# The second score matmul on 128 rows in place of 64, its low operand padded with zeros

## The chip, the cores and the metric

The kernel runs on one core of one Trainium2 chip. The metric is the time of one execution on the device, in microseconds (us); lower is better. Times are given as the median of several executions. A core has five engines that run their own queues of instructions: TensorE (PE in the profile; PEld is its weight loads), VectorE (DVE), ScalarE (ACT), GpSimd (POOL) and SyncE (SP, which only issues transfers here).

## The reference

One step of a hybrid decoder layer, for a prompt of 2048 tokens and a group of 8 × 8 sample tokens, with 1024 channels, in float32. Each token is normalised, projected into three parallel branches (attention, a short gated convolution, a spatial MLP on chunks of 128 positions), and the branches are gated, projected back and added to the input. The change touches the attention of the prompt, whose core is this:

```python
def _sink_attend(q, k, v, dist, valid, sinks):
    s = jnp.einsum("...qkgd,...skd->...kgqs", q, k).astype(jnp.float32) * (HEAD_DIM ** -0.5)
    s = s - _alibi_slopes()[:, :, None, None] * dist.astype(jnp.float32)
    s = jnp.where(valid, s, NEG_INF)
    ...
    e = jnp.exp(s - mx)
    prob = e / (e.sum(axis=-1, keepdims=True) + jnp.exp(sink - mx))
    return jnp.einsum("...kgqs,...skd->...qkgd", prob.astype(v.dtype), v)
```

There are 8 query heads in 2 key groups, 64 channels a head, and a block of 128 queries sees the 128 keys of its own block and the 128 of the block before. The contraction of a score is thus over 64 channels.

## The kernel before

The tokens are worked through in four super-blocks (called blocks here) of 4 prompt tiles of 128 tokens; the last takes the 64 sample tokens too, so that its large products run in two chunks of 288 columns instead of one of 512. A block has these phases, in this order: `kv_phase` and `q_phase` (the "natural" products, L285 to L287, tokens on partitions, 256 columns), then the large products with the channels on partitions (L176 to L178) for the attention's gate, `conv_phase`, `chunk_phase` (with a second stretch of natural products and the spatial products, L672 and L673), `gate_phase` and `out_phase`.

To keep float32 precision on a faster matmul type (fp32r), every operand is split: the high part is a cast by ScalarE (L167), the low part the rest by VectorE (L168). A product is then three matmuls, high by high, high by low and low by high. Weights come by transfers from SyncE's queue, and their split is ordered two weight tiles ahead of their use.

Attention is done in units of one query tile and one key group, 8 units in a block, 32 in all. A unit has stages: `queries` (transposes, L421, then the split into `hh` and `ll`), `scores` (L441 and L442), the softmax on VectorE and ScalarE (L444 to L461), `probs` (transposes, L466, and a split) and `values` (L473 and L474). TensorE's order is written by hand: while the large products go on, a counter of weight tiles advances (`tick`), and a stage is put between the products when its time has come (`later`): scores 1.75 weight tiles behind the unit's start, the probabilities at 3.5 and 4, a new unit every 2. So all the stages of a unit stand between the large products of `conv_phase` and its neighbours. VectorE, ScalarE and GpSimd get their order from a scheduler.

A score has its own form of the split. The key tile `kst` holds the high part of a key's 64 channels at partitions 0 to 63 and the low part at 64 to 127 (L331, L332). The high part `hh` of the query stands in both halves, so that L441, over 128 rows, gives high by high and high by low in one matmul. The low part `ll` of the query stands at partitions 0 to 63 only, and L442 adds low by high over these 64 rows. Both write the same stretch of the PSUM tile `sp`, head by head: eight matmuls in a unit, each with 256 key columns (128 in the first two units of block 0, which have no block before them).

`hh` and `ll` are stretches of `rbuf`, two sets of them in turn. `rbuf` takes the buffer with the tag "mh", which the first block's input (`xin`), the spatial operand (`vbuf`) and the high part of the merged branches (`m`, read to the end of `out_phase`) take at other times.

On GpSimd there are the pairs of operations that make 1/rms (`rstd`, L163 and L164: xr for the tokens, kr for the keys, qr for the queries, vr for the MLP) and a few constants. The scaling of the keys, L341 on VectorE, takes kr; L319 on TensorE transposes the result.

Of the kernel before, what the change touches and what calls it, by code (L numbers as in the profile page):

```python
# [16 lines left out]
P = 128  # L17
D = 1024
# [9 lines left out]
WE = 1024  # L28
# Weight units loaded, and split, ahead of their use
RAWS = 3  # L30
AHEAD = 2
# When the side work of an attention unit, and of the spatial products, is emitted:
# delays in weight tiles of the large products
UNIT_EVERY = 2.0
# [3 lines left out]

# Super-blocks of tokens: (first prompt tile, prompt tiles, column chunks, with the sample group)
SBS = [  # L40
# [8 lines left out]
def trunk_kernel(ctx: ExitStack, tc: tile.TileContext, A, O):  # L49
# [27 lines left out]

    # Work that runs beside the large products: each piece is emitted when the
    # products have advanced to its time, counted in weight tiles of 1024 x 128.
    clock = [0.0]  # L80
# [14 lines left out]

# [1 line left out]
    def order():  # L97
# [44 lines left out]

# [1 line left out]
    def const(name):  # L144
# [7 lines left out]

# [1 line left out]
    xh = res.tile([P, KT, TMAX], F32R, name="xh")  # L154
# [6 lines left out]
    def rstd(out, ssq, n, width):  # L161
        """out = (ssq / width + eps) ** -0.5"""
        nc.gpsimd.tensor_scalar(out, ssq, 1.0 / width, EPS, ALU.mult, ALU.add)  # L163
        nc.gpsimd.tensor_tensor(out, out, mhalf[: out.shape[0], :n], ALU.pow)  # L164
# [5 lines left out]
    def gemm_t(ps, w, kts, rh, rl, c0, c1):  # L170
        """ps[m, c0:c1] = w[k, m].T @ r[k, c0:c1], three exact partial products per k tile"""
        wh, wl = w
        o = ps[:, : c1 - c0]
        for k in range(kts):
            ws = slice(k * P, (k + 1) * P)
            nc.tensor.matmul(o, wh[:, ws], rh(k, c0, c1), start=k == 0, stop=False)  # L176
            nc.tensor.matmul(o, wh[:, ws], rl(k, c0, c1), start=False, stop=False)  # L177
            nc.tensor.matmul(o, wl[:, ws], rh(k, c0, c1), start=False, stop=k == kts - 1)  # L178
            if k % 2:
                tick((c1 - c0) / 512 * 0.25)  # L180
# [3 lines left out]
    def t_tiles(j, chunks):  # L184
        """For one 128-column tile of w_in: (psum, c0, c1) of each chunk"""
        w = take("wt", j)
        for c0, c1 in chunks:
            ps = ps_mm()
            gemm_t(ps, w, KT, *xr, c0, c1)
            yield ps[:, : c1 - c0], c0, c1  # L190

# [1 line left out]
    def xrstd(sb):  # L193
        """Pieces that build 1 / rms of the block's tokens, on all partitions"""
        t0, _, chunks, _ = SBS[sb]
        n = chunks[-1][1]
        tiles = [(c, min(c + P, n)) for c in range(0, n, P)]
        st = {"x": res.tile([P, 4 * TMAX], F32, tag="za", name="xbuf")}
        st["r"] = res.tile([P, TMAX], F32, tag="acc", name="acc")[:, :n]
        r = small.tile([P, 8], F32, tag="xr", name="xr")  # L200

        def piece(j, c0, c1):
            w = c1 - c0
            x = st["x"][:w, j % 2 * D:(j % 2 + 1) * D]
            nc.sync.dma_start(x, A["xn"][t0 * P + c0:t0 * P + c1])
            nc.scalar.activation(x, x, AF.Square, accum_out=r[:w, j:j + 1])

        def fin():
            for j0, j1, w in ((0, n // P, P), (n // P, len(tiles), n % P)):
                if w and j1 > j0:  # L210
                    rstd(r[:w, j0:j1], r[:w, j0:j1], j1 - j0, D)

        def spread():
            for t in (tiles[:4], tiles[4:]):
                if t:
                    ps = ps_tp()
                    b = t[0][0]
                    for c0, c1 in t:
                        w = c1 - c0
                        nc.tensor.transpose(  # L220
                            ps[:, c0 - b:c1 - b], r[:w, c0 // P:c0 // P + 1].broadcast_to([w, P]), ident[:w, :w]
                        )
                    nc.scalar.copy(st["r"][:, b:t[-1][1]], ps[:, : t[-1][1] - b])

        return st, [lambda j=j, c=c: piece(j, *c) for j, c in enumerate(tiles)] + [fin, spread]
# [21 lines left out]
    def first_block():  # L247
        """The first block's x, 128 tokens at a time so that the products start early"""
        xin = res.tile([P, 8 * TMAX], F32, tag="mh", name="xin")
        xnat = res.tile([P, 8 * TMAX], F32, tag="ml", name="xnat")  # L250
        r = small.tile([P, 8], F32, tag="xr", name="xr")
        rbuf = res.tile([P, 4 * TMAX], F32, tag="za", name="xrbuf")
        view = lambda t, i: t[:, i * D:(i + 1) * D].rearrange("p (k t) -> p k t", k=KT)  # noqa: E731

# [22 lines left out]

# [1 line left out]
    def natural(o, i, rows, units, n=256):  # L279
        """[rows tokens of tile i, n columns], the columns' weights in two units of 4 k tiles"""  # L280
        ts = slice(i * P, i * P + rows)
# [117 lines left out]

    def attention(sb, qn, abuf, za, br, start, every):  # L400
        """Schedules the block's attention: units of (128 queries, key group), each in stages"""
        t0, ntile, _, _ = SBS[sb]
        rbuf = res.tile([P, 4 * 1024], F32R, tag="mh", name="rbuf")
        sbuf = res.tile([P, 8 * TMAX], F32, tag="ml", name="sbuf")
        state = {}
# [11 lines left out]
        def queries(i, g, b):  # L417
            ps = ps_tp()
            q0 = i * 512 + g * 256
            for a in range(2):  # L420
                nc.tensor.transpose(ps[:, a * P:(a + 1) * P], qn[:, q0 + a * P:q0 + (a + 1) * P], ident)  # L421
            # head 2 a + e of the group has the channels at partitions 64 e
            hh = b["hh"].rearrange("p (a e t) -> p a e t", a=2, e=2)
# [10 lines left out]
        def scores(i, g, b, kbs):  # L434
# [3 lines left out]
            for h in range(4):  # L438
                rhs = kst[:, g, i + kbs[0]: i + 2, :]
                hs = slice(h * P, (h + 1) * P)  # L440
                nc.tensor.matmul(sp[:, h, k0:], b["hh"][:, hs], rhs, start=True, stop=False)  # L441
                nc.tensor.matmul(sp[:, h, k0:], b["ll"][:HD, hs], rhs[:HD], start=False, stop=True)  # L442
            for h in range(4):
# [53 lines left out]
    def sample_attention(samp, sbuf, za, br):  # L497
        """Schedules the attention of the sample group over the cached and the new keys"""
        cv, kc = sbuf[:, 2048:3072], sbuf[:, 3072:4096]
# [5 lines left out]
        def queries():  # L505
            q = samp["q"]
            ps = ps_tp()
            for h in range(8):
                nc.tensor.transpose(
                    ps[0:HD, h * NTS:(h + 1) * NTS], q[h // 4][:, (h % 4) * HD:(h % 4 + 1) * HD], ident[:NTS, :NTS]  # L510
                )
            # columns are (sequence, head of the group, token)
            for g in range(2):
# [108 lines left out]
    def chunk_phase(sb, br, samp_args):  # L622
# [24 lines left out]
        def mixed(i, rows, t, gg):  # L647
            """Times u * silu(z), for the channel groups gg"""
            ts = slice(i * P, i * P + rows)
            t = t[:, gg]  # L650
            nc.vector.tensor_tensor(t, t, suc[:, gg, ts], ALU.mult)
            split(br2[0][:, gg, ts], br2[1][:, gg, ts], t)
# [55 lines left out]
    def keep(new, old):  # L708
        """The rows of a cache that stay in the window"""
        tc.keep_in_program_order(nc.scalar.dma_start(O[new][:, : P - TS, :], A[old][:, TS:, :]))  # L710
# [83 lines left out]

    # spatial weights, transposed and masked: [s, group, t], zero where s > t
    # as (high, low, high) parts side by side
    wsp = consts.tile([P, 4, 3, P], F32R, name="wsp")
    wsd = consts.tile([NTS, 4, NTS], F32, name="wsd")

    def spatial_weights():  # L800
# [6 lines left out]
        nc.scalar.copy(wsp[:, :, 2], wsr)  # L807
        # the sample group's, block-diagonal: [64, group, 64]
        nc.gpsimd.memset(wsd, 0.0)
# [37 lines left out]
def _tiles(w):  # L847
    """[K, M] -> [M / 128, 128 (k), K / 128, 128 (m)] with the last two merged"""
    k, m = w.shape
    return w.reshape(k // P, P, m // P, P).transpose(2, 1, 0, 3).reshape(m // P, P, k)  # L850


def _layout(i):
# [11 lines left out]
    c = {n: w[:, at[j]:at[j + 1]] for j, n in enumerate(names)}  # L865
    # channel tile t of branch A: head t, then head 4 + t
    perm = np.concatenate([np.r_[t * HD:(t + 1) * HD, (4 + t) * HD:(5 + t) * HD] for t in range(4)])
# [9 lines left out]
    nat = [np.concatenate([c["k"], c["v"]], 1), c["q"][:, :256], c["q"][:, 256:], c["vc"][:, :256], c["vc"][:, 256:]]  # L877
    # [chunk, half of k, 128 (k), 4 k tiles, 256 columns]
    a["wn"] = np.stack([x.reshape(2, 4, P, 256).transpose(0, 2, 1, 3) for x in nat]).reshape(10, P, 1024)
# [10 lines left out]
    a["sinkb"] = np.broadcast_to(sk, (P, 8))  # L890
    # sample rows are (sequence mod 4, head of the group, token)
    a["sinks_s"] = np.tile(np.repeat(sk.reshape(2, 4).T, TS, 0), (4, 1))
# [9 lines left out]
    a["cv"] = cv.transpose(1, 0, 2, 3).reshape(P, NS * P)  # L902
    # tables that depend on shapes alone
    a["ident"] = np.eye(P, dtype=f)
# [49 lines left out]
```

## Time and profile before

| | |
|---|---|
| median of 3 runs | 2108.92 us (2108.08 to 2109.45) |
| span of the profiled execution, first to last instruction | 2107.5 us |
| time of the profiled execution outside its span | not recorded by itself; the median is 1.4 us above the span |
| TensorE busy | 2086.3 us, 99% |
| VectorE, ScalarE, GpSimd busy | 50%, 40%, 4% |
| mean granted clock of TensorE | 0.998 |
| matmuls of the scores, L441 and L442 | 128 each |

In the rows of the timeline the first number is the start in us from the beginning of the span, the second the duration in us; then follow the engine, the line, the operation, the output and the inputs. `64*128` in a matmul's row is the rows of the contraction by the columns of the loaded operand, `64x256` the moving operand. Brackets at the end give how long the engine idled ahead of the row and what ended that. Matmuls overlap and their ends are modelled, so their cost is read from start to start. In a row of windows the numbers are the stretch, its length, and the busy time of PE, PEld, DVE, ACT and POOL with instruction counts, then the granted clock, the share of the transfer engines and GB/s. A group's row gives the count, the busy us and the mean ns; one of a single line gives minimum, median and maximum in ns. A row of waits gives who waited for whom, the total in us, the times and the longest.

### The profile page before, as it was taken

How to read it: one execution, taken by the hardware profiler on the slowest of the kernel's cores; microseconds unless marked ns; L12 is line 12 of the kernel's file. 1: busy time of each engine (PE TensorE's matmuls, PEld its weight loads, DVE VectorE, ACT ScalarE, POOL GpSimd, SP SyncE). 2: the span in 40 equal slices, each digit the busy share in tenths (PEclk: the TensorE clock that was granted, in tenths of full speed). 3: DMA queues.
4: the chain of work that ended last, by engine and by line, in shares of the span. 5: the costliest groups of instructions: out<-in, count | busy, mean ns of one | idle time of the engine just before them, and what ended most of it. 6: DMA issues, size and time to landing. Idle time of an engine off the chain costs nothing.

```text
span 2107.5 us, 29115 instructions
## 1 busy us (share of the span) xinstructions
PE 2086.3 (99%) x11703; PEld 1808.5 (86%) x11703; DVE 1059.0 (50%) x1869; ACT 850.9 (40%) x1513; POOL 92.3 (4%) x160
## 2 busy tenths in 40 slices
PE   6999999999999999999999999999999999999999
PEld 6877888888877898888977788888899999999999
DVE  6576263335577444335467625334546852533332
ACT  5665243332566333333366524333346642323230
POOL 2100000000200000000200000000030000000000
PEclk9999999999999999999999999999999999999999
DMA  6222233436222223325422223333622241222233
GB/s 196 84 71 80 84 102 109 125 106 215 81 70 71 90 76 114 117 90 188 128 81 70 81 80 100 120 98 118 205 85 51 51 119 56 63 86 81 86 101 105
DMA packets 85703, 212.36 MB, mean 101 GB/s; under 512 B 18225, under 2 KB 23345, under 8 KB 85553
## 3 DMA queue, kind: packets, MB, share of 16 engines
q1 hardware_dynamic: 85536, 209.53, 32.2%
q8 instruction: 92, 1.51, 0.3%
q10 hardware_dynamic: 32, 0.98, 0.1%
q14 instruction: 43, 0.34, 0.1%
HBM read 201.46 MB, written 10.00 MB: 100 GB/s over the span
## 4 chain that ended last, share of the span: by engine, by line
PE 98%; ACT 1%; DVE 1%; DMA 0%; POOL 0%; issue 0%; SPq 0%; DVEq 0%
PE ps_mm L176 26%; PE ps_mm L177 26%; PE ps_mm L178 26%; PE ps_mm L287 3%; PE ps_mm L286 3%; PE ps_mm L285 3%; PE sp L442 2%; PE sp L441 2%; PE ps_tp L466 1%; PE first L286 1%; PE first L285 1%; PE first L287 1%; PE pv L473 1%; PE pv L474 1%; PE ps_tp L672 0%; PE ps_tp L673 0%
## 5 line engine op out<-in xcount | busy, mean ns | idle before, releaser
L176 PE MATMUL ps_mm<-xh,wh 128*128 128x512 f32 (+1 forms) x2080 | 752.6, 362 | 0.5 <-ACT za L828 0.5
L178 PE MATMUL ps_mm<-xh,wl 128*128 128x512 f32 (+1 forms) x2080 | 740.2, 356 | 0.0
L177 PE MATMUL ps_mm<-xl,wh 128*128 128x512 f32 (+1 forms) x2080 | 740.1, 356 | 0.0
L168 DVE TENSOR_TENSOR wl<-raw,wh 128x1024 fp32r<-128x1024 f32 x376 | 407.4, 1085 | 529.9 <-ACT wh L167 527.7
L167 ACT CAST wh<-raw 128x1024 fp32r<-128x1024 f32 x376 | 353.0, 940 | 763.8 <-PE ps_mm L177 593.2
L176 PEld LDWEIGHTS ps_mm<-xh,wh 128*128 128x128 f32 x2080 | 392.5, 189 | 56.8 <-ACT za L828 0.7
L178 PEld LDWEIGHTS ps_mm<-xh,wl 128*128 128x128 f32 x2080 | 392.5, 189 | 56.7
L177 PEld LDWEIGHTS ps_mm<-xl,wh 128*128 128x128 f32 x2080 | 393.0, 189 | 51.5
L285 PE MATMUL ps_mm<-wh,xh 128*128 128x256 f32 (+1 forms) x544 | 155.7, 286 | 5.3 <-ACT xh L167 5.3
L286 PE MATMUL ps_mm<-wl,xh 128*128 128x256 f32 (+1 forms) x544 | 153.3, 282 | 1.9 <-DVE wl L168 1.9
L287 PE MATMUL ps_mm<-wh,xl 128*128 128x256 f32 (+1 forms) x544 | 153.7, 282 | 0.9 <-DVE xl L168 0.9
L177 PE MATMUL ps_mm<-ml,wh 128*128 128x512 f32 (+1 forms) x320 | 112.5, 351 | 0.3 <-DVE ml L168 0.3
L178 PE MATMUL ps_mm<-mh,wl 128*128 128x512 f32 (+1 forms) x320 | 112.4, 351 | 0.0
L176 PE MATMUL ps_mm<-mh,wh 128*128 128x512 f32 (+1 forms) x320 | 112.3, 351 | 0.0
L740 DVE TENSOR_TENSOR t<-ps_mm,t 128x512 f32<-128x512 f32 (+1 forms) x120 | 71.5, 596 | 77.0 <-PE ps_mm L178 75.6
L285 PEld LDWEIGHTS ps_mm<-wh,xh 128*128 128x128 f32 (+1 forms) x544 | 102.0, 188 | 6.6 <-ACT xh L167 6.4
L286 PEld LDWEIGHTS ps_mm<-wl,xh 128*128 128x128 f32 (+1 forms) x544 | 102.0, 188 | 2.5 <-DVE wl L168 2.3
L287 PEld LDWEIGHTS ps_mm<-wh,xl 128*128 128x128 f32 (+1 forms) x544 | 101.8, 187 | 1.5 <-DVE xl L168 1.3
L724 ACT ACTIVATE t<-ps_mm,c_bg 128x512 f32<-128x512 f32 (+1 forms) x120 | 73.0, 609 | 72.4 <-PE ps_mm L178 72.3
L429 ACT ACTIVATE rbuf<-ps_tp,c_qnw 64x256 fp32r<-64x256 f32 x128 | 60.0, 469 | 23.8 <-PE ps_tp L421 12.4
L444 DVE SCALAR_TENSOR_TENSOR sbuf<-c_negdist,sp 128x256 f32<-128x256 f32 (+1 forms) x128 | 44.3, 407 | 48.0 <-PE sp L442 48.0
L177 PEld LDWEIGHTS ps_mm<-ml,wh 128*128 128x128 f32 x320 | 60.0, 188 | 8.0 <-DVE ml L168 0.6
(202 smaller groups left out, 2605.7 us busy)
## 6 DMA issues: line engine op xcount, KB each, us to landing
raw<-in_wt SPq DMA_DIRECT2D x208, 512.0 KB
raw<-in_wout SPq DMA_DIRECT2D x96, 256.0 KB
raw<-in_wn SPq DMA_DIRECT2D x40, 512.0 KB
raw<-in_wo SPq DMA_DIRECT2D x32, 512.0 KB
xbuf<-in_xn SPq DMA_DIRECT2D x12, 512.0 KB
xt<-in_xt SPq DMA_DIRECT2D x24, 256.0 KB
out_yt<-xt SPq DMA_DIRECT2D x24, 256.0 KB
xbuf<-in_xt SPq DMA_DIRECT2D x16, 256.0 KB
```

Of the source, the lines that this page charges most:

```text
L167: nc.scalar.copy(hi, src)
L168: nc.vector.tensor_tensor(lo, src, hi.bitcast(F32), ALU.subtract)
L176: nc.tensor.matmul(o, wh[:, ws], rh(k, c0, c1), start=k == 0, stop=False)
L177: nc.tensor.matmul(o, wh[:, ws], rl(k, c0, c1), start=False, stop=False)
L178: nc.tensor.matmul(o, wl[:, ws], rh(k, c0, c1), start=False, stop=k == kts - 1)
L285: nc.tensor.matmul(o, xh[:, k, ts], wh[:, ws], start=k == 0, stop=False)
L286: nc.tensor.matmul(o, xh[:, k, ts], wl[:, ws], start=False, stop=False)
L287: nc.tensor.matmul(o, xl[:, k, ts], wh[:, ws], start=False, stop=k == KT - 1)
L429: nc.scalar.activation(hh[half, :, e], src, AF.Copy, scale=qnw2[es])
L444: nc.vector.scalar_tensor_tensor(s[:, h, k0:], negdist[:, k0:], SLOPES[4 * g + h], sp[:, h, k0:], ALU.mult, ALU.add)
L724: nc.scalar.activation(t[:, c0:c1], pg[:, : c1 - c0], AF.Sigmoid, bias=bg[:, 8 * b + d:8 * b + d + 1])
L740: nc.vector.tensor_tensor(t[:, c0:c1], pa[:, : c1 - c0], t[:, c0:c1], ALU.mult)
```

## The change

The second score matmul takes all 128 rows of `ll` and of the keys. Its upper 64 rows of `ll`, which nothing else writes, are set to zero by GpSimd, once in a block for each of the two sets. So the low part of the query meets the high part of the key as before, and zeros meet the key's low part. Comments and docstrings are taken out too; from the two new lines on, the lines of the changed kernel stand 2 further down (L441 and L442 become L443 and L444).

```diff
         rbuf = res.tile([P, 4 * 1024], F32R, tag="mh", name="rbuf")
+        for p in range(2):
+            nc.gpsimd.memset(rbuf[HD:, p * 1024 + 512:(p + 1) * 1024].bitcast(F32), 0.0)
         sbuf = res.tile([P, 8 * TMAX], F32, tag="ml", name="sbuf")
...
                 nc.tensor.matmul(sp[:, h, k0:], b["hh"][:, hs], rhs, start=True, stop=False)
-                nc.tensor.matmul(sp[:, h, k0:], b["ll"][:HD, hs], rhs[:HD], start=False, stop=True)
+                nc.tensor.matmul(sp[:, h, k0:], b["ll"][:, hs], rhs, start=False, stop=True)
```

The order of the instructions on TensorE, VectorE, ScalarE and SyncE is the same in both kernels. On GpSimd the two memsets of each block come in. In block 0 (`kr` is 1/rms of a key tile, `ks` the sum of squares it comes from; lines with + are of the changed kernel):

```order
 L163 TENSOR_SCALAR kr<-ks 128x2 [waits DVE_49]
 L164 TENSOR_TENSOR kr<-kr,mhalf 128x2 [waits Pool_49]
-L163 TENSOR_SCALAR kr<-ks 128x2 [waits DVE_49]
+L405 MEMSET rbuf 64x512 [waits DMAHW3_49,DMAHW4_49,DMAHW1_49,DMAHW7_49,DVE_49,Pool_49]
+L405 MEMSET rbuf 64x512
+L163 TENSOR_SCALAR kr<-ks 128x2 [waits DVE_49,Pool_49]
 L164 TENSOR_TENSOR kr<-kr,mhalf 128x2 [waits Pool_49]
```

They stand ahead of the block's fourth and last kr, far ahead of the attention, and wait for the buffer's earlier user, the first block's input. At the start of block 1 on GpSimd (`xr` is 1/rms of the block's tokens):

```order
 L163 TENSOR_SCALAR xr<-xr 128x4 [waits Activation_49]
 L164 TENSOR_TENSOR xr<-xr,mhalf 128x4 [waits Pool_49]
-L163 TENSOR_SCALAR kr<-ks 128x2 [waits DVE_49]
+L405 MEMSET rbuf 64x512 [waits DVE_49,PE_49,Pool_49]
+L405 MEMSET rbuf 64x512
+L163 TENSOR_SCALAR kr<-ks 128x2 [waits DVE_49,Pool_49]
 L164 TENSOR_TENSOR kr<-kr,mhalf 128x2 [waits Pool_49]
```

Here, and in blocks 2 and 3, they stand ahead of the first kr and wait for TensorE, whose products of the block before read the same buffer. On TensorE the first score matmuls of block 0, before:

```order
L178 MATMUL ps_mm<-xh,wl 128x512
L441 MATMUL sp<-kst,rbuf 128x128 [waits Activation_49]
L442 MATMUL sp<-kst,rbuf 128x128 [waits DVE_49]
L441 MATMUL sp<-kst,rbuf 128x128 [waits Activation_49]
L442 MATMUL sp<-kst,rbuf 128x128 [waits DVE_49]
```

The same place in the changed kernel:

```order
L178 MATMUL ps_mm<-xh,wl 128x512
L443 MATMUL sp<-kst,rbuf 128x128 [waits Activation_49]
L444 MATMUL sp<-kst,rbuf 128x128 [waits DVE_49,Pool_49]
L443 MATMUL sp<-kst,rbuf 128x128 [waits Activation_49]
L444 MATMUL sp<-kst,rbuf 128x128 [waits DVE_49]
```

Nothing moved; the first L444 that reads a set of buffers waits for GpSimd as well.

## The prediction, made before the changed kernel ran

> **What bounds the kernel now.** I read the page of the profile first: how busy each engine is, and the chain of work that ended last.
>
> ```profile
> span 2107.5 us, 29115 instructions
> PE 2086.3 (99%) x11703; PEld 1808.5 (86%) x11703; DVE 1059.0 (50%) x1869; ACT 850.9 (40%) x1513; POOL 92.3 (4%) x160
> ...
> PE 98%; ACT 1%; DVE 1%; DMA 0%; POOL 0%; issue 0%; SPq 0%; DVEq 0%
> ```
>
> TensorE is busy for 99% of the span and is 98% of the last chain. So time goes where TensorE's instructions go, and a change on TensorE shows one for one unless a new wait eats it. The second view is what TensorE waited for, from 45 us to the end, that is without the start:
>
> ```profile
> PE ps_mm L176 <- ACT za L828: 0.5, 1, 0.5
> PE ps_mm L177 <- DVE ml L168: 0.3, 1, 0.3
> PE ps_tp L672 <- DVE sp L676: 0.2, 1, 0.2
> ```
>
> That is the whole answer: 1.0 us in 2062. No other engine holds TensorE up today, but these rows don't say how much room the others have left, and I come back to that.
>
> A busy engine can still be badly used, because a matmul's end in this trace is modelled. So the third view is TensorE's timeline, read by its start times. This is one attention unit of block 0, the eight score matmuls (L441 and L442 in turn, one pair a head) and the products behind them:
>
> ```profile
> 96.11 0.28 PE L441 MATMUL sp<-kst,rbuf 128*128 128x256 f32 x1
> 96.32 0.38 PE L442 MATMUL sp<-kst,rbuf 64*128 64x256 f32 x1
> 96.64 0.39 PE L441 MATMUL sp<-kst,rbuf 128*128 128x256 f32 x1
> ...
> 98.52 0.50 PE L176 MATMUL ps_mm<-xh,wh 128*128 128x512 f32 x1
> 98.85 0.40 PE L177 MATMUL ps_mm<-xl,wh 128*128 128x512 f32 x1
> ```
>
> The second starts 0.21 us behind the first; from there on one starts every (98.52 − 96.32) / 7 = 0.31 us: 128 rows, 64 rows, 128 rows. All eight together make 0.30 us each. The L176 behind them also keeps its successor waiting for 0.33 us. Beside this, the eight spatial matmuls (L672 and L673 in turn), which have the same 256 columns, the same type and the same pairing into one accumulation, but 128 rows every time:
>
> ```profile
> 283.64 0.28 PE L672 MATMUL ps_tp<-wsp,vbuf 128*128 128x256 f32 x1
> ...
> 284.48 0.28 PE L673 MATMUL ps_tp<-wsp,vbuf 128*128 128x256 f32 x1
> 284.59 0.40 PE L176 MATMUL ps_mm<-xh,wh 128*128 128x512 f32 x1
> 284.82 0.39 PE L177 MATMUL ps_mm<-xl,wh 128*128 128x512 f32 x1
> ```
>
> Eight of them take 284.59 − 283.64 = 0.95 us, 0.12 each, and the L176 behind them 0.23. Where is the difference spent? In the weight loads. The first fence gives the loads of the score matmuls as groups, and the first row of the second gives one load's start; the other rows are loads among 128-row matmuls in a natural product:
>
> ```profile
> L441 PEld LDWEIGHTS sp<-kst,rbuf x128: 186/186/191, 68.1 to 1681.3; 128*128 128x128 f32 x128
> L442 PEld LDWEIGHTS sp<-kst,rbuf x128: 182/183/183, 68.4 to 1681.6; 64*128 64x128 f32 x128
> ```
>
> ```profile
> 34.98 0.19 PEld L286 LDWEIGHTS ps_mm<-wl,xh 128*128 128x128 f32 x1
> 35.10 0.19 PEld L287 LDWEIGHTS ps_mm<-wh,xl 128*128 128x128 f32 x1
> ...
> 96.63 0.19 PEld L441 LDWEIGHTS sp<-kst,rbuf 128*128 128x128 f32 x1
> ```
>
> Among 128-row matmuls a load of 0.19 us starts every 0.12 us, so each runs under the matmul ahead of it. The load of the third score matmul starts at 96.63, where that matmul itself is recorded (96.64): it was not pulled ahead. Load and stream follow each other, 0.19 + 0.12 = 0.31 us, and that is the spacing seen. I conclude that what the kernel pays for here is each change between a 64-row and a 128-row matmul.
>
> **The change part by part.** *The second matmul on 128 rows.* All eight matmuls of a unit, and those ahead of and behind them, then have 128 rows. I price them by the spatial rows above: 0.95 for eight and 0.23 for the L176 behind. A full unit of blocks 0 to 2 takes 98.85 − 96.11 = 2.74 us now, and would take 1.18: 1.56 us less. Block 3 has 288 columns in its products and thus its own unit:
>
> ```profile
> 1632.49 0.28 PE L441 MATMUL sp<-kst,rbuf 128*128 128x256 f32 x1
> ...
> 1634.89 0.40 PE L176 MATMUL ps_mm<-xh,wh 128*128 128x288 f32 x1
> 1635.13 0.29 PE L177 MATMUL ps_mm<-xl,wh 128*128 128x288 f32 x1
> 1635.26 0.29 PE L178 MATMUL ps_mm<-xh,wl 128*128 128x288 f32 x1
> ```
>
> It takes 2.64 us; after, 0.95 + 0.13 (the spacing of its undisturbed products) = 1.08, again 1.56 less. The first two units of block 0 see only one key block, 128 columns:
>
> ```profile
> 68.30 0.22 PE L441 MATMUL sp<-kst,rbuf 128*128 128x128 f32 x1
> ...
> 70.23 0.50 PE L176 MATMUL ps_mm<-xh,wh 128*128 128x512 f32 x1
> 70.57 0.40 PE L177 MATMUL ps_mm<-xl,wh 128*128 128x512 f32 x1
> ```
>
> They take 2.27 us. No row has 128 such columns on 128 rows throughout. Not more than the 256-column price gives 1.18, a gain of 1.09; half of that per matmul would give 0.48 more. I take the 1.09, since a load of the same 128 columns stays, and keep the other for the range.
>
> Sum: 4 blocks of 8 units are 32; 2 are short, 8 lie in block 3, 22 remain. 22 × 1.56 = 34.3, 8 × 1.56 = 12.5, 2 × 1.09 = 2.2: together 49.0 us less on TensorE.
>
> The Trainium skill, "TensorE: Matmul & The Clock Gate", section "LDWEIGHTS (loading the stationary operand)", says that a load's time comes from its columns and not from the contraction rows; by that alone the row count is no lever and the sum would be 0. The rows agree on the load's length (183 against 186 ns), but the change is in when it starts, of which that section says nothing.
>
> *The zero rows.* Two memsets of 64x512 per block on GpSimd, eight in all, ahead of a block's first or fourth kr. The only memset of that kind in the trace has half the columns:
>
> ```profile
> L809 POOL MEMSET wsd<- 64x256 f32 x1 | 0.3, 304 | 0.0
> ```
>
> So one is between 0.30 and, at twice the columns, 0.61 us; I take 0.6, a pair 1.2. Behind it in GpSimd's queue stands kr, for which the keys' scaling (L341) on VectorE waits, and behind that TensorE's transposes (L319). In blocks 1 to 3 the pair waits for the last product of the block before (it reads the same buffer), in block 0 for the last of x:
>
> ```profile
> 518.88 0.40 PE L178 MATMUL ps_mm<-mh,wl 128*128 128x512 f32 x1
> ```
>
> ```profile
> 35.74 1.09 POOL L163 TENSOR_SCALAR kr<-ks 128x2 f32<-128x2 f32 x1 [2.76 <-DVE ks L299]
> ...
> 522.80 0.19 POOL L163 TENSOR_SCALAR kr<-ks 128x2 f32<-128x2 f32 x1 [140.77 <-DVE ks L299]
> ```
>
> From 518.88 + 0.40 to 522.80 are 3.5 us, and in block 0 GpSimd idles 2.76 us ahead of that kr. The pair fits in both: 0 us. The first L444 of each buffer now also waits for GpSimd, but the memset is over some 30 us earlier: 0. Were the cover gone, it would be at most 4 × 1.2 = 4.8 us. The order on VectorE, ScalarE, SyncE and TensorE stays, and no transfer is added.
>
> *What is late next.* The probabilities' transposes (L466) need the softmax of VectorE and ScalarE, which starts behind the scores. A usual unit, and then one of the tightest:
>
> ```profile
> 1110.01 1.41 DVE L444 SCALAR_TENSOR_TENSOR sbuf<-c_negdist,sp 128x256 f32<-128x256 f32 x4 [1.36 <-PE sp L442]
> ...
> 1118.75 1.14 DVE L461 TENSOR_SCALAR sbuf<-sbuf,den 128x256 f32<-128x256 f32 x4
> ...
> 1619.33 1.42 DVE L444 SCALAR_TENSOR_TENSOR sbuf<-c_negdist,sp 128x256 f32<-128x256 f32 x4 [0.48 <-PE sp L442]
> ...
> 1629.18 1.14 DVE L461 TENSOR_SCALAR sbuf<-sbuf,den 128x256 f32<-128x256 f32 x4
> ```
>
> ```profile
> 1121.38 0.38 PE L466 MATMUL ps_tp<-c_ident,sbuf 128*128 128x128 f32 x2
> ...
> 1630.47 0.60 PE L466 MATMUL ps_tp<-c_ident,sbuf 128*128 128x128 f32 x4
> ```
>
> Usual: the softmax ends at 1118.75 + 1.14 = 1119.89, 1.49 us ahead of L466. After, L466 comes 1.56 earlier, while the last score comes 7 × (0.30 − 0.12) = 1.27 earlier (VectorE, which idles 1.36 there, can follow). The room shrinks by 0.3, to 1.2: no wait. Tight: 1630.32 against 1630.47 leaves 0.15, and VectorE can start only 0.48 earlier, so TensorE would wait 1.56 − 0.48 − 0.15 = 0.93 us. Setting each unit's last L461 beside its next L466 in the same way, three of the 32 units have under half a microsecond of room (this one, and those at 96 and 1648 us). At 0.93 at most each that is 0 to 2.8 us; I take 2.
>
> Result: 2107.5 − 49.0 + 2 = 2060.5 as a span. The median of the three runs, 2108.92, lies 1.4 above the span; the profiled execution shows no other time of its own, so I add the same 1.4: **2061.9 us**.
>
> **The rivals.** *The spacing is not due to the rows.* If loads of the scores are not pulled ahead for another reason, and the 128-row L444 stays at 0.31, the time stays at 2108.9 us. For it: in the 64-row case too, half of the matmuls (L441) have 128 rows and pay. Against it: the first L441 of a unit, with a 128-row matmul ahead, is followed after 0.21 rather than 0.31, the L176 behind the last L442 pays as well, and the spatial pairs don't. The Trainium skill speaks for this rival on the same page, Part 3, "The mechanism": a load is pulled ahead of running matmuls only where its row group doesn't conflict (or it goes to the background weight buffer), and after the change both loads would fill all four groups; by the row-group half of that rule nothing is gained. The loads at 34.98 and 35.10, on all rows, overlap all the same. I give it 0.04.
>
> *VectorE becomes the bound in the attention stretches.* A pair of units:
>
> ```profile
> 1120.40:1151.80 31.40, 31.40 (x141) 24.21 (x141) 24.48 (x52) 20.14 (x43) 0.00 (x0) 1.00 0.21 67
> ```
>
> VectorE (24.48, the third pair of numbers) would have 31.40 − 3.12 = 28.28 us for it, 87%. It idles 6.92 today, of which about 2 × 1.36 goes with the earlier scores; the 4.2 left is just over the 3.8 that there would be. If the rest doesn't shrink, each of the 14 pairs loses 0.4, some 6 us. If the loss builds up and only half of the 49 gets through, the time is 2086. It decides once VectorE's own idling is above 3.8 us a pair. For 2072 to 2092 I give 0.07.
>
> *Slower: the memsets hold up kr.* With 3.5 us of room in a block, each microsecond beyond it delays the keys by one. To end above 2113.1 it would have to eat 47 + 4.2 = 51 us, 12.8 a block, so memsets of (3.5 + 12.8) / 2 = 8.2 us each, 13 times my estimate. At 10 us each: 4 × (20 − 3.5) = 66, less 47, is 2128 us. Nothing in the trace speaks for it but that short operations on GpSimd vary (0.19 and 1.09 us for the same kr above): 0.02.
>
> **How the numbers follow.** The forecast, all 128-row spacing with waits of a few microseconds, has 0.87. Its own range: without any wait and with the cheaper short units, 2061.9 − 2 − 1 = 2059, and 2 us for what one profiled execution leaves open, so 2057; upward, 0.3 us more in each of 30 full units, 9 us, to 2071, and 2072 with the short memset cover gone in one block. The range 2057 to 2072 holds about nine tenths of the 0.87, so 8 in 10; the rest of the case and the rivals are left out. The runs before differ by 0.07%; a difference of 0.2%, 4.2 us, is about what can be told from no change. Faster by more than that: the forecast and the VectorE case, 0.94. Within: 0.04. Slower: 0.02.
>
> **What would show it.** In the profile after, the second score matmul must stand as 128*128, score matmuls must start about 0.12 us apart, a unit must take 1.2 us, and TensorE's busy time must fall by about 49 us. If the unit stays at 2.7, the reading of the rows is wrong. If the unit is 1.2 and the time is above 2072, there must be waits of TensorE for L461 or for a weight split (L168), and they price it. A wait of L319 for L341 would show the memsets.

## The result and the profile after

The changed kernel takes 2060.98 us (median of 4, 2059.51 to 2061.16) against 2108.88 us before: a ratio of 0.9772, 95% interval 0.9759 to 0.9786. That is 47.9 us less, where 47.0 were forecast (2061.9 us).

The page of the changed kernel: busy times, and the chain that ended last.

```profile
span 2057.7 us, 29142 instructions
PE 2037.0 (99%) x11703; PEld 1794.7 (87%) x11703; DVE 1057.5 (51%) x1869; ACT 850.8 (41%) x1513; POOL 96.2 (5%) x168
...
PE 98%; ACT 1%; DVE 1%; DMA 0%; POOL 0%; issue 0%; SPq 0%; DVEq 0%
```

TensorE has as many matmuls as before and is busy 49.3 us less; the span is 49.8 us shorter. The other engines do what they did, GpSimd 3.9 us more. TensorE's timeline, the first unit with two key blocks (L443 is the high product, L444 the low one):

```profile
94.01 0.28 PE L443 MATMUL sp<-kst,rbuf 128*128 128x256 f32 x1
94.13 0.28 PE L444 MATMUL sp<-kst,rbuf 128*128 128x256 f32 x1
94.25 0.29 PE L443 MATMUL sp<-kst,rbuf 128*128 128x256 f32 x1
...
94.96 0.40 PE L176 MATMUL ps_mm<-xh,wh 128*128 128x512 f32 x1
95.20 0.39 PE L177 MATMUL ps_mm<-xl,wh 128*128 128x512 f32 x1
```

The eight now start 0.12 us apart, and the L176 behind them holds its successor up for 0.24 us and not 0.33. The unit takes 95.20 − 94.01 = 1.19 us, against 2.74. TensorE's weight loads at the same place, and their groups over the whole run:

```profile
94.02 0.19 PEld L444 LDWEIGHTS sp<-kst,rbuf 128*128 128x128 f32 x1
94.13 0.19 PEld L443 LDWEIGHTS sp<-kst,rbuf 128*128 128x128 f32 x1
```

```profile
L443 PEld LDWEIGHTS sp<-kst,rbuf x128: 186/189/193, 68.3 to 1632.9; 128*128 128x128 f32 x128
...
L444 PEld LDWEIGHTS sp<-kst,rbuf x128: 187/188/193, 68.5 to 1633.1; 128*128 128x128 f32 x128
```

The load of the low product has even grown by 5 ns, from 183 to 188. But the L444 load that starts at 94.02 is for the matmul of 94.13, and the next, at 94.13, for that of 94.25: each runs one matmul ahead. A unit is counted here from its first score matmul to the start of the second product behind it, as in the prediction. So counted, the 32 units took 85.9 us before and take 36.9 us now, summed from the start times of all: 49.0 us less.

### The profile page after: what moved, and what is told of

Same layout as the page of the kernel before. It is cut to its first block, busy times and chain, and to the rows that moved or that the text cites. A ratio compares the mean times of both kernels' runs of the same rounds, so it can differ in the third digit from the quotient of the medians.

```text
span 2057.7 us, 29142 instructions
## 1 busy us (share of the span) xinstructions
PE 2037.0 (99%) x11703; PEld 1794.7 (87%) x11703; DVE 1057.5 (51%) x1869; ACT 850.8 (41%) x1513; POOL 96.2 (5%) x168
## 3 DMA queue, kind: packets, MB, share of 16 engines
q8 instruction: 92, 1.51, 0.3%
## 4 chain that ended last, share of the span: by engine, by line
PE 98%; ACT 1%; DVE 1%; DMA 0%; POOL 0%; issue 0%; SPq 0%; DVEq 0%
PE ps_mm L176 27%; PE ps_mm L177 27%; PE ps_mm L178 27%; PE ps_mm L287 3%; PE ps_mm L285 3%; PE ps_mm L286 3%; PE ps_tp L468 1%; PE sp L444 1%; PE sp L443 1%; PE first L287 1%; PE first L286 1%; PE first L285 1%; PE pv L475 1%; PE pv L476 1%; PE ps_tp L674 0%; PE ps_tp L675 0%
## 5 line engine op out<-in xcount | busy, mean ns | idle before, releaser
L176 PE MATMUL ps_mm<-xh,wh 128*128 128x512 f32 (+1 forms) x2080 | 749.7, 360 | 0.5 <-ACT za L830 0.5
L176 PEld LDWEIGHTS ps_mm<-xh,wh 128*128 128x128 f32 x2080 | 392.6, 189 | 52.5 <-ACT za L830 0.7
L176 PE MATMUL ps_mm<-mh,wh 128*128 128x512 f32 (+1 forms) x320 | 112.5, 351 | 0.0
L431 ACT ACTIVATE rbuf<-ps_tp,c_qnw 64x256 fp32r<-64x256 f32 x128 | 60.0, 469 | 23.8 <-PE ps_tp L423 12.4
L176 PEld LDWEIGHTS ps_mm<-mh,wh 128*128 128x128 f32 x320 | 60.1, 188 | 7.5
```

The costliest lines, as they stand in the source:

```text
L431: nc.scalar.activation(hh[half, :, e], src, AF.Copy, scale=qnw2[es])
```

## The experiments

The theory on trial (A): a change between a 64-row and a 128-row matmul has a fixed price, and nothing else about the score matmuls has one. The rivals are named in the expectations.

**Another order, without zeros (e1_pairs).** The kernel before, with two high products in a row and then two low ones:

```diff
-            for h in range(4):
-                rhs = kst[:, g, i + kbs[0]: i + 2, :]
-                hs = slice(h * P, (h + 1) * P)
-                nc.tensor.matmul(sp[:, h, k0:], b["hh"][:, hs], rhs, start=True, stop=False)
-                nc.tensor.matmul(sp[:, h, k0:], b["ll"][:HD, hs], rhs[:HD], start=False, stop=True)
+            rhs = kst[:, g, i + kbs[0]: i + 2, :]
+            for h0 in range(2):
+                for h in (h0, h0 + 2):
+                    hs = slice(h * P, (h + 1) * P)
+                    nc.tensor.matmul(sp[:, h, k0:], b["hh"][:, hs], rhs, start=True, stop=False)
+                for h in (h0, h0 + 2):
+                    hs = slice(h * P, (h + 1) * P)
+                    nc.tensor.matmul(sp[:, h, k0:], b["ll"][:HD, hs], rhs[:HD], start=False, stop=True)
```

> The kernel before with the same eight score matmuls in another order: the high products of heads 0 and 2, then their 64-row low products, then the same for heads 1 and 3. Nothing is padded. A unit then has 4 changes between 128 and 64 rows (the last one into the products behind it) in place of 8. Theory A, a fixed price for each change (1.56 / 8 = 0.195 us): a unit takes 1.18 + 4 x 0.195 = 1.96 us, the time is 2061 + 32 x 0.78 = 2086 us, and the second of two 64-row matmuls starts 0.12 us behind the first. Theory B, a 64-row load is never pulled ahead, nor is a load behind one: 6 exposed loads, 2.35 us a unit, 2098 us, and the second 64-row matmul starts 0.31 us behind the first. Theory C, the 64-row matmul is slow because it adds to what its own high product has just written: nothing of it is left once another matmul stands between, 2061 us.

2084.79 us, ratio 0.9885 (0.9870 to 0.9900). A unit in its timeline (L442 is the high product, L445 the low one), where `x2` merges two matmuls into a row:

```profile
110.07 0.39 PE L442 MATMUL sp<-kst,rbuf 128*128 128x256 f32 x2
110.39 0.50 PE L445 MATMUL sp<-kst,rbuf 64*128 64x256 f32 x2
110.82 0.50 PE L442 MATMUL sp<-kst,rbuf 128*128 128x256 f32 x2
111.25 0.49 PE L445 MATMUL sp<-kst,rbuf 64*128 64x256 f32 x2
111.68 0.50 PE L176 MATMUL ps_mm<-xh,wh 128*128 128x512 f32 x1
```

Half the changes, half the gain, with four 64-row matmuls a unit as before. A gave 2086 us, B 2098, C 2061. A pair takes 0.43 us between two changes; two bare matmuls would take 0.24. So 0.19 us belong to one change. Neither theory had the place right: inside a row the second 64-row matmul starts at 110.61, 0.22 us behind the first, where A gave 0.12 and B 0.31. Its load starts at 110.50, 0.11 us ahead of it, so a 64-row load as such is pulled ahead. The load of the first 64-row matmul starts at 110.39, with its matmul: it is the load behind a change that is not. A unit with 64 rows throughout, the high product cut in two as well, was not tried.

**The 64-row product twice (e2_low_twice).** The low product of each head is issued a second time, so it counts double in the scores:

```diff
-                nc.tensor.matmul(sp[:, h, k0:], b["ll"][:HD, hs], rhs[:HD], start=False, stop=True)
+                nc.tensor.matmul(sp[:, h, k0:], b["ll"][:HD, hs], rhs[:HD], start=False, stop=False)
+                nc.tensor.matmul(sp[:, h, k0:], b["ll"][:HD, hs], rhs[:HD], start=False, stop=True)
```

> The kernel before with each 64-row low product issued twice in a row (so the low part counts double in the scores). The number of changes between 128 and 64 rows stays at 8 a unit. Theory A: four more matmuls at 0.12 us, 0.48 us a unit, 2109 + 15 = 2124 us, and the second copy starts 0.12 us behind the first. Theory B: each copy pays its load, 4 x 0.31 = 1.25 us a unit, 2149 us.

2133.12 us (ratio 1.0118, 1.0102 to 1.0135), between the two forecasts. The timeline tells which part is which (L443 is the copy):

```profile
114.59 0.28 PE L441 MATMUL sp<-kst,rbuf 128*128 128x256 f32 x1
114.80 0.38 PE L442 MATMUL sp<-kst,rbuf 64*128 64x256 f32 x1
115.02 0.28 PE L443 MATMUL sp<-kst,rbuf 64*128 64x256 f32 x1
115.22 0.38 PE L441 MATMUL sp<-kst,rbuf 128*128 128x256 f32 x1
115.54 0.38 PE L442 MATMUL sp<-kst,rbuf 64*128 64x256 f32 x1
```

A head takes 115.54 − 114.80 = 0.74 us against 0.63 before, so the extra 64-row matmul costs 0.11, not 0.31. All units together grew by 15 us (85.9 to 100.8), which is A's figure. What A had wrong is where the price falls. The copy starts 0.22 us behind, not 0.12: about half of a change's price lies behind the matmul ahead of the change (0.21 in place of 0.12) and half behind the one after it (0.22). Where changes follow each other at once, as in the kernel before, each gap has both halves, 0.31.

The other 9 to 10 us (7.8 between the two profiled executions) are no part of the scores. The mean granted clock is 0.993 here against 0.998 before. Windows from the end of a unit of block 1 on (the third number from the end is the granted clock):

```profile
620.00:624.00 4.00, 4.00 (x15) 3.14 (x15) 2.63 (x5) 1.04 (x1) 0.00 (x0) 0.68 0.00 0
624.00:628.00 4.00, 4.00 (x18) 3.18 (x18) 2.61 (x5) 3.89 (x5) 0.00 (x0) 0.89 0.13 19
```

The clock falls in some stretches of this kernel where that of the kernel before stays at 1.00. With TensorE busy throughout, (0.998 − 0.993) × 2130 is some 10 us, the size of the remainder. That the added 64-row matmuls lower the clock is likely by this, but no run tries it by itself.

**One head of four (e3_one_head).** The changed kernel with head 1 back on 64 rows:

```diff
-                nc.tensor.matmul(sp[:, h, k0:], b["ll"][:, hs], rhs, start=False, stop=True)
+                n = HD if h == 1 else P
+                nc.tensor.matmul(sp[:, h, k0:], b["ll"][:n, hs], rhs[:n], start=False, stop=True)
```

> The changed kernel, but head 1's low product on 64 rows as before; the other three heads stay on 128. A unit has 2 changes in place of 0 or 8. Theory A: 1.18 + 2 x 0.195 = 1.57 us a unit, 2061 + 32 x 0.39 = 2073.5 us, and only the two starts behind the changes are late. Theory D, a unit pays as a whole once it holds a change at all: 2.7 us a unit, 2109 us.

2072.88 us, ratio 0.9829 (0.9815 to 0.9844); A gave 2073.5, D 2109. Its timeline round the one 64-row matmul (L443 is the high product, L445 the low one):

```profile
94.18 0.28 PE L445 MATMUL sp<-kst,rbuf 128*128 128x256 f32 x1
94.30 0.28 PE L443 MATMUL sp<-kst,rbuf 128*128 128x256 f32 x1
94.51 0.38 PE L445 MATMUL sp<-kst,rbuf 64*128 64x256 f32 x1
94.83 0.38 PE L443 MATMUL sp<-kst,rbuf 128*128 128x256 f32 x1
95.05 0.28 PE L445 MATMUL sp<-kst,rbuf 128*128 128x256 f32 x1
95.16 0.28 PE L443 MATMUL sp<-kst,rbuf 128*128 128x256 f32 x1
```

The gaps are 0.12, 0.21, 0.32, 0.22, 0.11: beside 0.12 each, that is 0.09 + 0.20 + 0.10 = 0.39 us for two changes, and the three neighbours share it. "Only the two starts behind the changes are late" was wrong in the same way as in the run before: three are, by the same sum. Zero, two, four and eight changes in a unit gave 2061, 2073, 2085 and 2109 us, 12 us for every two.

**96 rows (e4_rows96).** The changed kernel with the low product on 96 rows, 32 of them zero:

```diff
-                nc.tensor.matmul(sp[:, h, k0:], b["ll"][:, hs], rhs, start=False, stop=True)
+                nc.tensor.matmul(sp[:, h, k0:], b["ll"][:96, hs], rhs[:96], start=False, stop=True)
```

> The changed kernel with the low product on 96 rows: 64 of the query's low part and 32 zero rows. Theory A in the form that the price is for a change between the 64-row and the 128-row division of the array: 96 rows are more than 64 and need the full division, no change, 2061 us. Theory E, any change in the number of rows costs: 2109 us.

2060.97 us, ratio 0.9771 (0.9757 to 0.9786): as the changed kernel. The starts of a unit:

```profile
93.99 0.28 PE L443 MATMUL sp<-kst,rbuf 128*128 128x256 f32 x1
94.11 0.29 PE L444 MATMUL sp<-kst,rbuf 96*128 96x256 f32 x1
94.23 0.29 PE L443 MATMUL sp<-kst,rbuf 128*128 128x256 f32 x1
94.36 0.28 PE L444 MATMUL sp<-kst,rbuf 96*128 96x256 f32 x1
```

So it is not that the number of rows differs, but that one is at 64. The Trainium skill, "TensorEngine Tiling (Array Packing)", section "Tiling Modes", lists divisions of the array into 128, 64 or 32 rows, and says that a change of the division drains TensorE; it gives no price. These runs agree with it, with 0.19 us for a change, and with 96 rows counting as 128. Whether TensorE empties at a change or only the next load is held back, no run here separates; a change costs about what the load takes (0.18 to 0.19 us). Fewer than 64 rows were not tried.

**The zeros alone (e5_zeros_alone).** The changed kernel with its memsets, but the low product on 64 rows as before:

```diff
-                nc.tensor.matmul(sp[:, h, k0:], b["ll"][:, hs], rhs, start=False, stop=True)
+                nc.tensor.matmul(sp[:, h, k0:], b["ll"][:HD, hs], rhs[:HD], start=False, stop=True)
```

> The changed kernel with the two memsets of each block kept, but the low product on 64 rows as before. Theory A: all of the gain comes from the rows and none from another order or pace on GpSimd, so 2109 us as before, within 2 us. Rival F, part of the 48 us comes with the memsets: clearly under 2105 us.

2108.58 us, ratio 0.9998 (0.9988 to 1.0007). Within that interval, some 2 us, the memsets neither cost nor bring anything.

**The sample group's small products.** The clock in e2 made me look where the granted clock of the changed kernel falls. It does so from the middle of the value products of the sample group on, 64 matmuls with 32 columns in one run from 1707.2 to 1715.5 us (the expectation says behind that run). In this run they go in four parts between the large products; the work is the same (e6_sample_spread):

```diff
-        later(5.0, values)
+        for j in range(4):
+            later(5.0 + 0.5 * j, lambda a=(j // 2, j % 2 * 4): values(*a))
```

> The changed kernel with the 64 small value products of the sample group (L573, L574; 32 columns each, in one run of some 9 us) put between the large products in four runs of 16, half a weight tile apart. In the profile of the changed kernel the granted clock falls to one half for some 7 to 10 us behind that run. Theory G, the clock falls because the run keeps TensorE thinly occupied for longer than the throttle looks back: the low clock there is gone, 3.4 to 5 us less, 2056 to 2057.5 us. Rival H, the fall is not due to that run: 2061 us and the low clock stays.

2057.08 us, ratio 0.9755 (0.9740 to 0.9769), against 0.9772 for the changed kernel. Windows of the changed kernel, then of this run:

```profile
1706.00:1712.00 6.00, 6.00 (x53) 4.99 (x51) 0.29 (x1) 0.41 (x1) 0.00 (x0) 1.00 0.28 90
1712.00:1718.00 6.00, 6.00 (x33) 5.33 (x32) 0.85 (x2) 0.40 (x1) 0.00 (x0) 0.52 0.00 0
1718.00:1724.00 6.00, 6.00 (x43) 6.00 (x43) 1.31 (x2) 1.35 (x2) 0.00 (x0) 0.91 0.03 2
```

```profile
1706.00:1712.00 6.00, 6.00 (x48) 5.51 (x47) 0.43 (x1) 0.41 (x1) 0.00 (x0) 1.00 0.29 90
1712.00:1718.00 6.00, 6.00 (x49) 5.19 (x47) 1.23 (x1) 1.35 (x2) 0.00 (x0) 1.00 0.25 87
```

The half clock (0.52 over six microseconds) is gone, and 3.9 us of the time with it, as G gave. The two ratios' intervals overlap, but the slowest execution here (2057.53) is below the fastest of the changed kernel (2059.51). So the fall belongs to these products standing in one run; why such a run lowers the clock, G's second half, is argued and not shown.

**And on 128 rows (e7_sample_rows).** Each pair of those products has one over 128 cached keys and one over the 64 new ones. Here the second has 128 rows too, with zeros in both operands:

```diff
-                nc.tensor.matmul(o, vs[:, gs], pts[0:NTS, 256 + c:256 + c + 32], start=False, stop=True)
+                nc.tensor.matmul(o, vs[:, gs], pts[:, 256 + c:256 + c + 32], start=False, stop=True)
...
+                nc.gpsimd.memset(vs[NTS:], 0.0)
...
+            nc.gpsimd.memset(pts[NTS:, 256:512], 0.0)
```

> As the run with the sample's value products spread, and in each pair of them the second product on 128 rows in place of 64, with zero rows that GpSimd writes (64x128 and twice 64x256). They alternate between 128 and 64 rows as the prompt's scores did, and start 0.115 us apart at full clock. Theory A: 64 of them at half that spacing or less, 3 to 4 us below the spread version, 2052.5 to 2054.5 us. Rival I, float32 products with 32 columns are 0.115 us apart for another reason: no difference to the spread version.

2053.77 us, ratio 0.9740 (0.9726 to 0.9755), the lowest of all; its interval lies under that of the changed kernel. The starts in e6 and then in e7. Each of the 32 float32 products stands in the trace as two matmuls, merged to a row:

```profile
1707.31 0.30 PE L574 MATMUL yps<-sbuf 128*64 128x32 f32 x2
1707.54 0.30 PE L575 MATMUL yps<-sbuf,abuf 64*64 64x32 f32 x2
1707.77 0.30 PE L574 MATMUL yps<-sbuf 128*64 128x32 f32 x2
```

```profile
1708.92 0.28 PE L577 MATMUL yps<-sbuf,abuf 128*64 128x32 f32 x2
1709.04 0.28 PE L576 MATMUL yps<-sbuf 128*64 128x32 f32 x2
1709.15 0.28 PE L577 MATMUL yps<-sbuf,abuf 128*64 128x32 f32 x2
```

From 0.23 us for two to 0.12, over 64 matmuls 3.5 us; measured 3.3 us between the two runs. There is one change to a row, so a change costs 0.11 us here, with 64 columns loaded in place of 128 (a load takes 0.13 to 0.14 us). The same lever works in another place, on plain float32 and with 32 columns. These products were not run on 128 rows without being spread, so whether their changes of rows have a part in the fall of the clock stays open.

## Why the prediction held, and the one term that didn't

**TensorE sets the time: right.** It is 98% of the last chain in both kernels, and what the units lost (49.0 us by their start times) the span lost (49.8 us); the 0.8 more are taken up below.

**The price of the rows: right, to the first decimal.** 2.74 to 1.18 was forecast for a full unit, 2.74 to 1.19 came; the two short units gained 1.15 each, where 1.09 was taken. The comparison that carried it was the spatial products, which have the columns, the type and the pairing of the scores, on 128 rows. Grouped durations would have misled: L441 went from a median of 385 ns and L442 from 382 to about 280 each, 0.1 us, while the starts moved by 0.19. As for the mechanism, the step "load and stream follow each other, 0.19 + 0.12" gave the right sum for two adjoining changes. Runs e1 to e3 show it in more detail: 0.09 to 0.10 us is lost on each side of a change, and only the load behind a change starts with its matmul rather than ahead of it.

**The rivals.** That the spacing had another cause fell with e1, e3 and e4, which change nothing but where and whether 64-row matmuls stand: e1 has as many 64-row matmuls as before, e3 a quarter of them, e4 none. VectorE did not become the bound. TensorE's waits from 45 us to the end of the changed kernel:

```profile
PE ps_mm L176 <- ACT za L830: 0.5, 1, 0.5
PE ps_mm L177 <- DVE ml L168: 0.3, 1, 0.3
PE ps_tp L674 <- DVE sp L678: 0.2, 1, 0.2
```

They are the three of before, and as long. The memsets take 0.52 us each (0.6 was taken), and e5 prices them at nothing. On GpSimd of the changed kernel:

```profile
508.27 0.98 POOL L405 MEMSET rbuf<- 64x512 f32 x2 [137.29 <-PE ps_mm L178]
511.42 0.19 POOL L163 TENSOR_SCALAR kr<-ks 128x2 f32<-128x2 f32 x1 [2.16 <-DVE ks L299]
```

They end 2.16 us ahead of the kr that they stand before here, and 1.73 us in block 0, where the room is least.

**The 2 us of new waits: wrong, they are 0.** The step was "VectorE can start only 0.48 earlier, so TensorE would wait 1.56 − 0.48 − 0.15 = 0.93 us". It took the end of the softmax to follow the start of its first VectorE operation. The same tight unit in the changed kernel, on VectorE, then ScalarE, then TensorE:

```profile
1577.80 1.41 DVE L446 SCALAR_TENSOR_TENSOR sbuf<-c_negdist,sp 128x256 f32<-128x256 f32 x4
...
1586.26 0.17 DVE L460 TENSOR_TENSOR den<-den,es 128x4 f32<-128x4 f32 x1 [3.67 <-ACT es L459]
...
1586.68 1.14 DVE L463 TENSOR_SCALAR sbuf<-sbuf,den 128x256 f32<-128x256 f32 x4
```

```profile
1580.07 0.95 ACT L431 ACTIVATE rbuf<-ps_tp,c_qnw 64x256 fp32r<-64x256 f32 x2 [1.17 <-PE ps_tp L423]
...
1584.06 0.51 ACT L454 ACTIVATE sbuf<-sbuf,nm 128x256 f32<-128x256 f32 x1
```

```profile
1587.96 0.60 PE L468 MATMUL ps_tp<-c_ident,sbuf 128*128 128x128 f32 x4
```

VectorE waits 3.67 us for the exponentials. They stand in ScalarE's queue behind L431, which splits the next unit's queries and waits for their transposes (L423), and those stand on TensorE behind the scores. When the scores get shorter, the transposes come earlier by as much, and the whole chain with them. So the room ahead of the probabilities' transposes (L468) is set by TensorE at both ends. In this unit and two others it doesn't depend on how long the scores take (times by start, to within 0.01 us):

| kernel | that unit, us | room there | sixth unit of block 3 | fourth unit of block 2 |
|---|---|---|---|---|
| before | 2.63 | 0.15 | 0.48 | 1.49 |
| e1_pairs | 1.86 | 0.15 | 0.47 | 1.51 |
| e3_one_head | 1.48 | 0.14 | 0.47 | 1.50 |
| changed | 1.09 | 0.14 | 0.48 | 1.49 |

Set side by side in the same way, 29 of the 32 units keep their room to within 0.02 us; the late chain was read in the tight one alone. The last unit of block 3, which has no next unit, does lose room with shorter scores (2.99 to 1.54 us), and so do the first two of block 0 (8.1 to 6.9 and 9.4 to 7.8): there the room shrinks as the prediction reckoned, and enough is left.

That the forecast missed by only 0.9 us, with 2 us too many in it, is in part luck: two errors went the other way. Time minus span is 1.8 to 1.9 us in the four executions, where I had added 1.4 from a median and the span of another execution. And the median execution's span is 2059.2 us, 0.7 above the 2058.5 that the sum gives without waits. Spans are 2059.1 to 2059.3 in three executions and 2057.7 in the profiled one. Those three have no trace of their own, but e4_rows96, which runs as fast, has a span of 2059.0 us:

```profile
1706.00:1712.00 6.00, 6.00 (x47) 5.03 (x45) 0.45 (x1) 0.41 (x1) 0.00 (x0) 0.87 0.27 90
1712.00:1718.00 6.00, 6.00 (x34) 5.06 (x33) 0.48 (x2) 0.40 (x1) 0.00 (x0) 0.50 0.00 0
1718.00:1724.00 6.00, 6.00 (x39) 6.00 (x38) 1.31 (x2) 1.36 (x2) 0.00 (x0) 0.78 0.00 0
```

Taken as stretches at one half, these windows make (0.13 + 0.50 + 0.22) × 6 / 0.5 = 10.2 us, where the changed kernel's make (0.48 + 0.09) × 6 / 0.5 = 6.8. From the last unit to the end e4 takes 425.4 us, the changed kernel 424.3, the kernel before 425.3 (0.86, 0.50 and 0.79 in its windows from 1756 us on, again 10.2 us). So the profiled execution had the shorter stretch of low clock, and this was worth about 1.1 us. It covers the 0.8 us that the span lost beyond the units, and it is the likely, not shown, reason why the other three took some 1.5 us longer.

## What to carry to other kernels

Matmuls over 64 rows among matmuls over 128 pay for every crossing: here 0.19 us, one and a half times the price of the matmul itself, and 0.11 us in the sample's products. Pad the small one with zero rows if they can be written out of the way, or put the small ones next to each other. Read such a price from start to start and beside a stretch that differs in one thing only. Before costing a new wait, follow the late chain back to what releases its last step: if that is the engine that gets faster, the wait need not come.

## What the runs showed of the hardware beyond that

A TensorE that the profile shows as busy throughout can still be given half its clock: in and behind a run of 64 matmuls with 32 columns (0.52 in the six microseconds from 1712 us on), and in some places of e2 with more 64-row matmuls (0.68 and 0.89 from 620 to 628 us, which make 3.4 us at one half). Spreading that run over four places kept the clock at 1.00 and was worth 3.9 us. The Trainium skill, "TensorE: Matmul & The Clock Gate", Part 1, says that the clock is halved or restored by how busy the array was in windows of about 3.4 us; the granted clock of one half, the low stretches of 3.4, 6.8 and 10.2 us and the effect of spreading agree with it, and the same rows show that the busy share of the profile isn't the measure that it goes by.
